# Down projection of a hybrid decoder layer: four units loaded and split in another order, their buffers on the other stack, and one operand sum moved from GpSimd to VectorE

## The chip, the cores and the metric

The kernel runs on one core of a Trainium2 chip. The metric is the device time of one execution in microseconds (us); less is better. Three executions of the kernel before took 1797.55, 1800.30 and 1800.89 us, the median is 1800.3.

## What is computed

One decoder layer on 1024 tokens of width 1024, all in float32. Two token mixers (sparse attention and latent attention) come first; the change does not touch them. Behind them stands the channel mixer, to which every edit belongs:

```python
h = _rmsnorm(x, g_pre_ffn[i])
u = _causal_dwconv(h @ w_up[i], w_conv[i], b_conv[i])   # (1024, 5632), 3 taps along the tokens
a, v = u[..., :D_FF], u[..., D_FF:]                     # D_FF = 2816
x = x + _rmsnorm((jax.nn.gelu(a) * v) @ w_down[i], g_post_ffn[i])
```

A gated embedding `w_ple_gate` ends the layer.

## The kernel before

**Arithmetic.** A float32 product is made of three passes of a rounded type: each operand is split into a high part (a copy on ScalarE, L198) and a low part (a subtraction on VectorE, L199), both by `split_evac`, and `mm3` issues high x high (L193), low x high (L194) and high x low (L195). So an operand is ready for TensorE only when ScalarE and then VectorE have been over it.

**Up projection.** The 2816 channels are 22 chunks of 128 (`NF`), each with two halves (gate and value). Chunk 0 is multiplied plainly; chunks 1 to 21 use the Strassen-Winograd scheme, seven products P1 to P7 instead of eight. Its right operands T1 to T4 are sums of blocks of h (T2 = B22 - T1, T3 = T2 - B11, T4 = B21 - T2). `t_blocks` (L1239) makes them once, behind chunk 0's products: T2 and T3 on VectorE through `total` (L1249), T4 on GpSimd (L1258, L1265), each in two halves of 128 x 1024, split by `put`. `hh`, `hl` are high and low parts of h, `rh`, `rl` those of a weight block, which `prep` splits (from `wraw` or a sum `S0` to `S3` made by `block_sum`, L1179). Each chunk's seven results are combined in VectorE into `C` (L1354 to L1370), and `conv_pieces` (L1278) applies the convolution: on each half one ScalarE instruction (L1285) and two taps on VectorE (L1289), then gelu, the product (L1296) and a store of 128 x 1024 to DRAM (`g_d`, L1297). The pieces of chunk f run among the products of chunk f+1; those of the last chunk run in a loop of their own behind the last product.

**Down projection.** Again seven products, in the order P1, P5, P6, P3, P7, P4, P2, over 11 units each (`UNITS`, 128 channels of `g_d` with their rows of `w_down`). `load(n)` issues a unit's transfers on SyncE's queue, `ready(n)` makes its sums on VectorE (L1435) and splits it into `whi`, `wlo`, and `down_product` (L1474) issues twelve matmuls a unit, three passes for each of four banks. It calls `ready(n + 4)` and `load(n + 7)` behind unit n. `QA` holds the units of P1, `QS` and `GB` those of P5 and the sums for P6, P3 and P7. Split units have four homes in turn: two in `W.parts`, two in `ring2`.

**Memory and order.** Buffers come from pools on two stacks, left and right; a pool that is opened over a closed one has to wait for the readers of what stood there. In the kernel before, `ep` (C, u) and `ring` (split weights) on the left and `tp`, `hp` (T blocks, h) on the right are closed behind the last convolution; then `yacc` (the sum of the output), `ring2` and `qs` are opened on the left and `qa` on the right (L1458 to L1464). A scheduler of the compiler sets the order of instructions on each engine from the order of the program, the pools and its own cost estimates, so an instruction may stand earlier on its engine than in the code: units 0 and 1 of the first down product, split behind the last convolution in the code, have their low words among the last up products on VectorE, at 1406.01 and 1409.54 us of the span. Within an engine the order is then fixed.

Of the kernel before, what the change touches and what calls it, by code (L numbers as in the profile page):

```python
# [18 lines left out]
D = 1024  # L19
# [5 lines left out]
NF = FF // 128  # L25
# [8 lines left out]
def dap(t, off, dims):  # L34
    return bass.AP(tensor=t.tensor, offset=t.offset + off, ap=[list(d) for d in dims])
# [130 lines left out]
def tile_hybrid_layer(ctx: ExitStack, tc: tile.TileContext, x, p, positions, g_pre_mix, w_in,  # L166
# [4 lines left out]
    nc = tc.nc  # L171
# [91 lines left out]
    g_d = [dram([128, T], F32, f"g_d{f}") for f in range(NF)]  # L263
# [30 lines left out]
    hp = Pool("hp", side="right")  # L294
# [351 lines left out]
    QA = [q0([128, 8, 512], F32R, "QA0"), q1([128, 8, 512], F32R, "QA1")]  # L646
# [444 lines left out]
    ps2 = Pool("ps2", space=PSUM)  # L1091
# [12 lines left out]
    ring = Pool("ring", side="left")  # L1104
# [29 lines left out]
    T1 = []  # L1134
# [64 lines left out]
    for t in (4, 5, 6, 7, 0, 1, 2, 3):  # L1199
        c, lt = t // 4, slice(t % 4 * 128, t % 4 * 128 + 128)  # L1200
# [37 lines left out]

    def t_blocks():  # L1239

        parts, t1, t2, b21 = [slice(0, 2), slice(2, 4)], T1, {}, {}

        def of(n, ks):
            return [f32(b[:, ks]) for b in BB[n]]

        def total(eng, tag, first, *rest):
            sum_ = W.parts([128, 2, 512], F32, tag, bufs=2)
            for op, b in rest:
                eng.tensor_tensor(sum_, first, b, op=op)  # L1249
                first = sum_  # L1250
            return sum_

        def put(n, ks, src):
            split_evac(BB[n][0][:, ks], BB[n][1][:, ks], src)

        for j, ks in enumerate(parts):
            b21[j] = ep([128, 2, 512], F32, "u", bufs=3)
            nc.gpsimd.tensor_tensor(b21[j], *of("B21", ks), op=OP.add)  # L1258
        for j, ks in enumerate(parts):
            put("T1", ks, t1[j])  # L1260
        for j, ks in enumerate(parts):
# [117 lines left out]
    DOWN = ("P1", "P5", "P6", "P3", "P7", "P4", "P2")  # L1379
    NJ = NF // 2  # L1380
    UNITS = [(p_, j) for p_ in DOWN for j in range(NJ)]
    QA, QS, GB, LOADED = {}, {}, {}, {}
    A_ = {"A11": (0, 0), "A12": (0, 1), "A21": (1, 0), "A22": (1, 1)}
    unit = {}

    def fetch(dst, name, j):

        r, c = int(name[1]) - 1, int(name[2]) - 1
        if name[0] == "A":
            nc.sync.dma_start(dst, g_d[c * NJ + j][:, r * 512:(r + 1) * 512])  # L1390
        else:
            nc.sync.dma_start(dst, dap(w_down, (r * NJ + j) * 128 * D + c * 512, [[D, 128], [1, 512]]))

    def temp():
        return wpool([128, 2, 512], F32, "wraw", bufs=3)

    def load(n):
        if n >= len(UNITS):
            return
        p_, j = UNITS[n]  # L1400
        if p_ == "P1":
            q = temp() if n < 3 else qa([128, 2, 512], F32, f"QA{j}")
            fetch(q[:, 0], "A11", j)
            fetch(q[:, 1], "B11", j)
            if n >= 3:
                QA[j] = q
        elif p_ == "P5":
            if j < 3:
                QA[j] = qa([128, 2, 512], F32, f"QA{j}")
                fetch(QA[j][:, 0], "A11", j)  # L1410
                fetch(QA[j][:, 1], "B11", j)
            q = QS[j] = qs([128, 2, 512], F32, f"QS{j}")
            GB[j] = qa([128, 512], F32, f"GB{j}")
            fetch(q[:, 1], "B12", j)
            fetch(GB[j], "A21", j)
            fetch(q[:, 0], "A22", j)
        elif p_ == "P7":
            q = QA[j]
        else:
            q = temp()  # L1420
            for i, name in enumerate({"P6": (None, "B22"), "P3": ("A12", "B22"), "P4": ("A22", "B21"),
                                      "P2": ("A12", "B21")}[p_]):
                if name:
                    fetch(q[:, i], name, j)
        LOADED[n] = q

    def ready(n):

        if n >= len(UNITS):
            return  # L1430
        p_, j = UNITS[n]
        q = LOADED.pop(n)

        def total(out_, a, b, op):
            nc.vector.tensor_tensor(out_, a, b, op=op)  # L1435

        sub, a, s = OP.subtract, QA.get(j), QS.get(j)
        if p_ == "P5":
            total(s[:, 1], s[:, 1], a[:, 1], sub)
            total(s[:, 0], GB[j], s[:, 0], OP.add)  # L1440
        elif p_ == "P6":
            total(s[:, 0], s[:, 0], a[:, 0], sub)
            total(s[:, 1], q[:, 1], s[:, 1], sub)
            q = s
        elif p_ == "P3":
            total(q[:, 0], q[:, 0], s[:, 0], sub)
        elif p_ == "P7":
            total(a[:, 0], a[:, 0], GB[j], sub)
            total(a[:, 1], s[:, 1], a[:, 1], sub)
        elif p_ == "P4":  # L1450
            total(q[:, 1], q[:, 1], s[:, 1], sub)
        pool = W.parts if n % 4 < 2 else ring2
        unit[n] = [pool([128, 2, 512], F32R, tag, bufs=2) for tag in ("whi", "wlo")]
        split_evac(*unit[n], q)
# [19 lines left out]
    def down_product(pi, per_unit):  # L1474
# [108 lines left out]
    for n, t in enumerate(ORDER):  # L1583
# [33 lines left out]
        else:  # L1617
# [45 lines left out]
```

## Time and profile before

| what | value |
|---|---|
| median of three executions | 1800.3 us |
| profiled execution | 1800.91 us, of which the span 1799.2 us |
| granted TensorE clock, mean | 0.984 |
| TensorE busy | 1728.0 us (96%) |
| VectorE busy | 1201.3 us (67%) |
| ScalarE busy | 838.8 us (47%) |
| GpSimd busy | 319.6 us (18%) |

TensorE is busy almost throughout, so time is found where it is idle or where its clock is below full speed. The positions of the stretches in the span: T blocks 1005 to 1060, the up projection's loop to 1438, the boundary to the down projection 1438 to 1458, the second and third down products 1463 to 1530. In the rows, PE is TensorE, DVE VectorE, ACT ScalarE, POOL GpSimd, SP SyncE and SPq its DMA queue; "x4" behind an operation joins four of them into one row.

### The profile page before, as it was taken

What the parts mean: (1) busy time and instruction counts of PE and PEld (TensorE: products, weight loads), DVE (VectorE), ACT (ScalarE), POOL (GpSimd) and SP (SyncE); (2) the same over time, 40 slices, a digit from 0 to 9 for tenths busy, and PEclk for the clock granted to TensorE, in tenths of its full rate; (3) what the DMA queues carried; (4) which work ended last, traced back from release to release, by engine and by line L of the source; (5) the groups of instructions that cost most, each with busy time, mean ns of one, the idle gap of its engine ahead of it and who ended that gap; (6) DMA issues with size and microseconds to landing.
All of it is one profiled execution on the core that took longest, in us unless ns stands there. A gap on an engine that the chain in (4) does not pass through costs nothing. (4 is left out here: it accounts for less than half of the span.)

```text
span 1799.2 us, 23461 instructions
## 1 busy us (share of the span) xinstructions
PE 1728.0 (96%) x8585; PEld 1414.3 (79%) x8585; DVE 1201.3 (67%) x1871; ACT 838.8 (47%) x1498; POOL 319.6 (18%) x471
## 2 busy tenths in 40 slices
PE   8989999999999999998999899999999979999998
PEld 7878888887787787887778678888888757887886
DVE  6544431117888787777764888888888679768443
ACT  6442322126777676676532434444444343335321
POOL 3132000004555543333211200000000000001010
PEclk8999999999999999999999999999999989999999
DMA  5394213310002226656462022232222282438111
GB/s 193 89 276 122 58 37 93 102 58 24 1 1 66 89 83 172 164 151 180 129 219 82 24 82 71 82 94 70 84 92 76 99 317 82 149 117 275 57 59 47
DMA packets 182511, 191.94 MB, mean 107 GB/s; under 512 B 12804, under 2 KB 136124, under 8 KB 182396
## 3 DMA queue, kind: packets, MB, share of 16 engines
q1 hardware_dynamic: 175292, 180.91, 32.6%
q10 hardware_dynamic: 7104, 9.54, 1.7%
q8 instruction: 68, 1.11, 0.3%
q14 instruction: 47, 0.39, 0.1%
HBM read 142.96 MB, written 47.45 MB: 106 GB/s over the span
## 5 line engine op out<-in xcount | busy, mean ns | idle before, releaser
L235 POOL TENSOR_SCALAR stat<-stat 128x1 f32<-128x1 f32 (+1 forms) x48 | 18.0, 374 | 892.0 <-ACT yn L1130 622.0
L198 ACT ACTIVATE ph<-pT 128x512 fp32r<-128x512 f32 (+1 forms) x244 | 130.4, 556 | 61.6 <-PE pT L734 53.8
L199 DVE TENSOR_TENSOR pl<-pT,ph 128x512 fp32r<-128x512 f32 (+1 forms) x244 | 149.6, 629 | 14.2 <-ACT ph L198 12.6
L193 PE MATMUL pT<-hh,whi 128*128 128x512 f32 x384 | 150.8, 393 | 2.7 <-DVE Vc L199 1.5
L195 PE MATMUL pT<-hh,wlo 128*128 128x512 f32 x384 | 150.4, 392 | 0.0
L194 PE MATMUL pT<-hl,whi 128*128 128x512 f32 x384 | 150.1, 391 | 0.0
L195 PE MATMUL big<-hh,rl 128*128 128x512 f32 x364 | 142.1, 391 | 3.6 <-DVE rl L199 3.6
L193 PE MATMUL big<-hh,rh 128*128 128x512 f32 x364 | 142.8, 393 | 2.5 <-ACT C L1352 1.4
L194 PE MATMUL big<-hl,rh 128*128 128x512 f32 x364 | 142.4, 391 | 0.0
L718 DVE TENSOR_REDUCE mx<-sc 128x1 f32<-128x640 f32 (+7 forms) x128 | 106.6, 835 | 34.4 <-PE sc L797 24.7
L107 DVE TENSOR_TENSOR wlo<-wraw,whi 128x1024 fp32r<-128x1024 f32 x26 | 31.9, 1226 | 138.3 <-ACT whi L106 138.1
L1289 DVE SCALAR_TENSOR_TENSOR u<-C,wcT,u 128x1024 f32<-128x1024 f32 x88 | 110.8, 1279 | 4.7 <-ACT u L1285 4.7
L194 PE MATMUL big<-wlo,whi 128*128 128x512 f32 x242 | 98.4, 407 | 9.0 <-DVE wlo L199 9.0
L193 PE MATMUL big<-whi 128*128 128x512 f32 x242 | 93.2, 401 | 9.8 <-ACT whi L198 9.8
L195 PE MATMUL big<-whi,wlo 128*128 128x512 f32 x242 | 96.4, 398 | 0.0
L198 ACT ACTIVATE rh<-S 128x512 fp32r<-128x512 f32 x84 | 52.5, 628 | 92.1 <-PE big L194 78.8
L193 PEld LDWEIGHTS pT<-hh,whi 128*128 128x128 f32 x384 | 72.5, 189 | 18.7 <-DVE Vc L199 1.6
L198 ACT ACTIVATE rh<-wraw 128x512 fp32r<-128x512 f32 x67 | 41.8, 630 | 92.4 <-PE big L194 44.2
L195 PEld LDWEIGHTS pT<-hh,wlo 128*128 128x128 f32 x384 | 72.4, 189 | 15.4
L194 PEld LDWEIGHTS pT<-hl,whi 128*128 128x128 f32 x384 | 72.5, 189 | 15.0
L195 PEld LDWEIGHTS big<-hh,rl 128*128 128x128 f32 x364 | 68.8, 189 | 18.4 <-DVE rl L199 4.0
L193 PEld LDWEIGHTS big<-hh,rh 128*128 128x128 f32 x364 | 68.6, 189 | 18.5 <-ACT C L1352 2.3
(485 smaller groups left out, 4791.9 us busy)
## 6 DMA issues: line engine op xcount, KB each, us to landing
wraw<-in_w_up_dram SPq DMA_DIRECT2D x44, 512.0 KB, 3.8
wraw<-in_w_in_dram SPq DMA_DIRECT2D x24, 512.0 KB, 4.2
g<-gm_d SPq DMA_DIRECT2D x48, 256.0 KB, 3.5
wraw<-in_w_down_dram SPq DMA_DIRECT2D x47, 256.0 KB, 3.2
g_d<-u SPq DMA_DIRECT2D x22, 512.0 KB, 3.4
wraw<-g_d SPq DMA_DIRECT2D x36, 256.0 KB, 3.0
xt<-in_x_dram SPq DMA_DIRECT2D x16, 512.0 KB, 7.0
gm_d<-gms ACTq DMA_DIRECT2D x16, 512.0 KB, 3.0
```

Of the source, the lines that this page charges most:

```text
L107: nc.vector.tensor_sub(lo, raw, f32(hi))
L193: nc.tensor.matmul(ps, lh, rh, start=start, stop=False, skip_group_check=more)
L194: nc.tensor.matmul(ps, lh, rl, start=False, stop=False, skip_group_check=more)
L195: nc.tensor.matmul(ps, ll, rh, start=False, stop=stop, skip_group_check=more)
L198: nc.scalar.activation(hi, ps, AF.Copy)
L199: nc.vector.tensor_sub(lo, ps, f32(hi))
L235: nc.gpsimd.tensor_scalar(st, st, EPS, None, op0=OP.add)
L718: nc.vector.tensor_reduce(u.nm[:, r:r + 1], src, axis=AX.XY, op=OP.max, negate=True)
L1289: nc.vector.scalar_tensor_tensor(u[s], C[s][:, 2 - sh:2 - sh + T], wcT[:, 2 - sh, ch:ch + 1], u[s], op0=OP.mult, op1=OP.add)
```

## The change

Two edits. First, T4 is summed on VectorE by `total`, as T2 and T3 are, in the buffers `whi`, `wlo` of `W.parts`; the four GpSimd instructions and their two `u` buffers go. T4's sum is now two instructions for each half, four in all.

Second, the down projection's functions move ahead of the up loop, and within the last chunk (f = 21) `load(0)` to `load(2)` are issued at the third product and `ready(0)`, `ready(1)` at the fifth and sixth. Behind the up loop only `tp` and `hp` are closed; `ring2`, `yacc` and `qa` are opened on the right, over them, all eleven `QA` at once in the order 0, 1, 2, 10, 3 to 9. The last convolution no longer stands ahead of the down projection: its pieces run behind units 0, 1 and 2 of the first down product, `ready` ahead of them, and `ep` and `ring` are closed behind unit 3, where `qs` and a new pool `gb` are opened on the left. `per_unit` is called ahead of `load(n + 7)`.

```diff
     def t_blocks():
-        for j, ks in enumerate(parts):
-            b21[j] = ep([128, 2, 512], F32, "u", bufs=3)
-            nc.gpsimd.tensor_tensor(b21[j], *of("B21", ks), op=OP.add)
...
             put("T2", ks, t2[j])
-            nc.gpsimd.tensor_tensor(b21[j], b21[j], t2[j], op=OP.subtract)
...
         for j, ks in enumerate(parts):
-            put("T4", ks, b21[j])
+            b21h, b21l = of("B21", ks)
+            put("T4", ks, total(nc.vector, ("whi", "wlo")[j], b21h, (OP.subtract, t2[j]), (OP.add, b21l)))
...
+            if f == NF - 1 and s == 2:
+                for i in range(3):
+                    load(i)
+            if f == NF - 1 and s in (4, 5):
+                ready(s - 4)
         pieces = conv_pieces(f, C)
-    for runs in pieces:
-        for run in runs:
-            run()
...
-    for n in range(3):
-        load(n)
-    for pl in (ep, ring, tp, hp):
+    for pl in (tp, hp):
         pl.close()
-    yp = Pool("yp", side="left")
+    ring2 = Pool("ring2", side="right")
+    yp = Pool("yp", side="right")
     yacc = yp([128, NT, D], F32, "yacc")
-    ring2 = Pool("ring2", side="left")
-    qs = Pool("qs", side="left")
     qa = Pool("qa", side="right")
+    for j in (0, 1, 2, 10) + tuple(range(3, 10)):
+        QA[j] = qa([128, 2, 512], F32, f"QA{j}")
     for n in range(3, 7):
         load(n)
-    for n in range(4):
+    for n in (2, 3):
         ready(n)
...
             ready(n + 4)
+            per_unit(j)
             load(n + 7)
-            per_unit(j)
...
-    for pi in range(5):
+    def last_conv(j):
+        nonlocal qs, gb
+        if j < 3:
+            for run in pieces[2 * j] + pieces[2 * j + 1]:
+                run()
+        if j == 3:
+            for pl in (ep, ring):
+                pl.close()
+            qs, gb = Pool("qs", side="left"), Pool("gb", side="left")
+
+    down_product(0, last_conv)
+    for pi in range(1, 5):
         down_product(pi, nothing)
```

**VectorE in the T stretch.** Each row is line, operation, what it writes from what, and its size; the digits behind a name tell buffers apart. `S` are weight sums, `rl` low words of weights, `C10` and `U3` parts of the combined result. In the kernel before, behind the last T3 split:

```order
L1179 TENSOR_TENSOR S2_10216<-wraw_9780,wraw_9870 128x512
L1360 TENSOR_TENSOR U2_10259<-one_10241,e1_10174 128x512
L1179 TENSOR_TENSOR S1_10192<-S0_10169,wraw_9780 128x512
L1296 TENSOR_TENSOR u_10218<-u_10171,u_10218 128x1024
L1362 TENSOR_TENSOR C10_9986<-big_10152,U2_10259 128x512
L1179 TENSOR_TENSOR S3_10238<-wraw_9780,S1_10192 128x512
L199 TENSOR_TENSOR rl_10255<-S1_10192,rh_10254 128x512
L199 TENSOR_TENSOR rl_10277<-S2_10216,rh_10276 128x512
L1363 TENSOR_TENSOR C10_9986<-C10_9986,U3_10220 128x512
L199 TENSOR_TENSOR rl_10298<-S0_10169,rh_10297 128x512
```

In the changed kernel (its lines are shifted: L1293 is the convolution's product, L1436 and L1437 are combinations):

```order
L1179 TENSOR_TENSOR S2_10216<-wraw_9780,wraw_9870 128x512
L1249 TENSOR_TENSOR whi_10142<-hh1_9059,whi_10122 128x1024
L1179 TENSOR_TENSOR S1_10192<-S0_10169,wraw_9780 128x512
L1249 TENSOR_TENSOR wlo_10147<-hh1_9059,wlo_10127 128x1024
L1293 TENSOR_TENSOR u_10218<-u_10171,u_10218 128x1024
L1436 TENSOR_TENSOR C10_9986<-big_10152,U2_10259 128x512
L1249 TENSOR_TENSOR whi_10142<-whi_10142,hl1_9060 128x1024
L1179 TENSOR_TENSOR S3_10238<-wraw_9780,S1_10192 128x512
L199 TENSOR_TENSOR rl_10255<-S1_10192,rh_10254 128x512
L1249 TENSOR_TENSOR wlo_10147<-wlo_10147,hl1_9060 128x1024
L199 TENSOR_TENSOR rl_10277<-S2_10216,rh_10276 128x512
L199 TENSOR_TENSOR rl_10298<-S0_10169,rh_10297 128x512
```

The same kinds of rows stand there still (the order of a few has turned), and among them the four new sums of T4, at L1249.

**VectorE at the boundary between the projections.** `wlo` from `wraw` is unit 2 of the first down product, from `QA3` unit 3, from `QA4` unit 4. Before:

```order
L1354 TENSOR_TENSOR C10_9986<-big_13110,U2_13151 128x512
L1289 SCALAR_TENSOR_TENSOR u_13230<-C10_9986,wcT_85,u_13230 128x1024
L1289 SCALAR_TENSOR_TENSOR u_13235<-C11_9987,wcT_85,u_13235 128x1024
L1289 SCALAR_TENSOR_TENSOR u_13230<-C10_9986,wcT_85,u_13230 128x1024
L1289 SCALAR_TENSOR_TENSOR u_13235<-C11_9987,wcT_85,u_13235 128x1024
L199 TENSOR_TENSOR wlo_13310<-QA4_13270,whi_13309 128x1024
L199 TENSOR_TENSOR wlo_13329<-QA5_13273,whi_13328 128x1024
L1296 TENSOR_TENSOR u_13235<-u_13230,u_13235 128x1024
L199 TENSOR_TENSOR wlo_13288<-wraw_13247,whi_13287 128x1024
L199 TENSOR_TENSOR wlo_13292<-QA3_13267,whi_13291 128x1024
```

After (L1286 is a tap, L1293 the product, L1428 the combination):

```order
L1428 TENSOR_TENSOR C10_9986<-big_13110,U2_13151 128x512
L199 TENSOR_TENSOR wlo_13279<-wraw_13180,whi_13278 128x1024
L1286 SCALAR_TENSOR_TENSOR u_13304<-C10_9986,wcT_85,u_13304 128x1024
L1286 SCALAR_TENSOR_TENSOR u_13327<-C11_9987,wcT_85,u_13327 128x1024
L1286 SCALAR_TENSOR_TENSOR u_13304<-C10_9986,wcT_85,u_13304 128x1024
L199 TENSOR_TENSOR wlo_13283<-QA3_13263,whi_13282 128x1024
L1286 SCALAR_TENSOR_TENSOR u_13327<-C11_9987,wcT_85,u_13327 128x1024
L199 TENSOR_TENSOR wlo_13301<-QA4_13264,whi_13300 128x1024
L199 TENSOR_TENSOR wlo_13324<-QA5_13265,whi_13323 128x1024
L1293 TENSOR_TENSOR u_13327<-u_13304,u_13327 128x1024
```

Unit 2's low words move from behind the four taps and the product to a place ahead of them, and unit 3's to a place ahead of the last tap.

**VectorE in the second down product.** Between the low words of its units 3 and 4 (`QS3`, `QS4`), before:

```order
L199 TENSOR_TENSOR wlo_13529<-QS3_13463,whi_13528 128x1024
L1435 TENSOR_TENSOR QA0_13389<-QA0_13389,GB0_13393 128x512
L1435 TENSOR_TENSOR QA0_13389<-QS0_13392,QA0_13389 128x512
L199 TENSOR_TENSOR wlo_13559<-QS4_13486,whi_13558 128x1024
L1435 TENSOR_TENSOR QS2_13440<-QS2_13440,QA2_13437 128x512
L1435 TENSOR_TENSOR QS2_13440<-wraw_13694,QS2_13440 128x512
L1435 TENSOR_TENSOR QA1_13413<-QA1_13413,GB1_13417 128x512
L1435 TENSOR_TENSOR QA1_13413<-QS1_13416,QA1_13413 128x512
L1435 TENSOR_TENSOR QS3_13463<-QS3_13463,QA3_13267 128x512
L1435 TENSOR_TENSOR QS3_13463<-wraw_13714,QS3_13463 128x512
L199 TENSOR_TENSOR wlo_13582<-QS5_13509,whi_13581 128x1024
```

After:

```order
L199 TENSOR_TENSOR wlo_13532<-QS3_13466,whi_13531 128x1024
L1355 TENSOR_TENSOR QS5_13512<-GB5_13513,QS5_13512 128x512
L1355 TENSOR_TENSOR QS2_13443<-QS2_13443,QA2_13261 128x512
L1355 TENSOR_TENSOR QS2_13443<-wraw_13697,QS2_13443 128x512
L1355 TENSOR_TENSOR QS6_13535<-QS6_13535,QA6_13266 128x512
L1355 TENSOR_TENSOR QA1_13260<-QA1_13260,GB1_13421 128x512
L1355 TENSOR_TENSOR QA1_13260<-QS1_13420,QA1_13260 128x512
L1355 TENSOR_TENSOR QS6_13535<-GB6_13536,QS6_13535 128x512
L1355 TENSOR_TENSOR QS7_13565<-QS7_13565,QA7_13267 128x512
L199 TENSOR_TENSOR wlo_13562<-QS4_13489,whi_13561 128x1024
```

Between `QS3` and `QS4` two sums became eight, those of the units and products that follow; before, they stood further behind.

## Rows read from the trace of the kernel before

**Rows 1.** The page's first line.

```profile
span 1799.2 us, 23461 instructions
```

**Rows 2.** Busy time by stretch: us of each engine (instructions), granted clock, DMA.

```profile
1005.00:1060.00 55.00, 44.78 (x174) 33.98 (x172) 54.85 (x56) 28.65 (x36) 10.98 (x4) 0.94 0.16 48
1100.00:1420.00 320.00, 320.00 (x1413) 265.00 (x1413) 267.97 (x348) 144.51 (x200) 0.00 (x0) 1.00 0.26 85
1438.00:1458.00 20.00, 9.65 (x27) 6.59 (x26) 12.55 (x11) 8.27 (x8) 0.00 (x0) 0.66 1.03 380
1463.00:1530.00 67.00, 62.35 (x264) 48.40 (x263) 66.79 (x92) 27.38 (x30) 0.00 (x0) 1.00 0.38 132
```

**Rows 3.** Timeline of PE, 1010 to 1060: start, us, operation [idle before <-releaser].

```profile
1018.53 0.54 PE L195 MATMUL big<-hh,rl 128*128 128x512 f32 x1 [3.60 <-DVE rl L199]
...
1056.57 0.50 PE L193 MATMUL one<-T3h,rh 128*128 128x512 f32 x1 [1.47 <-DVE C L1370]
```

**Rows 4.** Timeline of POOL, 1004 to 1023.

```profile
1005.04 5.06 POOL L1258 TENSOR_TENSOR u<-hh,hl 128x1024 f32<-128x1024 f32 x2 [4.62 <-DVE hl L199]
1014.73 3.20 POOL L1265 TENSOR_TENSOR u<-u,whi 128x1024 f32<-128x1024 f32 x1 [4.63 <-DVE whi L1249]
```

**Rows 5.** Timeline of DVE, 1004 to 1024.

```profile
1004.87 0.42 DVE L1150 TENSOR_TENSOR whi<-whi,hl 128x256 f32<-128x256 f32 x1
1005.20 2.62 DVE L1150 TENSOR_TENSOR wlo<-wlo,hl 128x256 f32<-128x256 f32 x1
1007.75 3.43 DVE L1249 TENSOR_TENSOR whi<-hh,whi 128x1024 f32<-128x1024 f32 x1
1011.10 1.21 DVE L1249 TENSOR_TENSOR wlo<-hh,wlo 128x1024 f32<-128x1024 f32 x1
...
1015.64 2.83 DVE L199 TENSOR_TENSOR rl<-wraw,rh 128x512 fp32r<-128x512 f32 x1
...
1020.14 3.42 DVE L1249 TENSOR_TENSOR whi<-whi,hh 128x1024 f32<-128x1024 f32 x1
```

**Rows 6.** Timeline of PE, 1437 to 1458.

```profile
1437.94 0.39 PE L195 MATMUL big<-hh,rl 128*128 128x512 f32 x1
1446.21 1.22 PE L193 MATMUL big<-whi 128*128 128x512 f32 x2 [7.87 <-ACT whi L198]
1449.91 0.79 PE L194 MATMUL big<-wlo,whi 128*128 128x512 f32 x1 [2.48 <-DVE wlo L199]
...
1457.90 0.39 PE L193 MATMUL big<-whi 128*128 128x512 f32 x1
```

**Rows 7.** Timeline of DVE and ACT, 1438 to 1444.

```profile
1438.44 0.69 DVE L1354 TENSOR_TENSOR C<-big,U 128x512 f32<-128x512 f32 x1 [5.80 <-PE big L195]
...
1439.17 2.37 ACT L1285 ACTIVATE u<-C,wcT 128x1024 f32<-128x1024 f32 x2 [3.91 <-DVE C L1354]
...
1440.44 4.87 DVE L1289 SCALAR_TENSOR_TENSOR u<-C,wcT,u 128x1024 f32<-128x1024 f32 x4 [1.31 <-ACT u L1285]
...
1441.45 1.99 ACT L198 ACTIVATE whi<-QA 128x1024 fp32r<-128x1024 f32 x2
```

**Rows 8.** Timeline of SP's queue and of DVE, 1448 to 1464.

```profile
1448.75 0.32 SPq L1297 DMA_DIRECT2D g_d<-u  x1
...
1463.21 0.69 DVE L1435 TENSOR_TENSOR QS<-QS,QA 128x512 f32<-128x512 f32 x1 [6.32 <-DMA QS<-in_w_down_dram]
```

**Rows 9.** Timeline of DVE, 1478 to 1481.

```profile
1478.76 1.22 DVE L199 TENSOR_TENSOR wlo<-QS,whi 128x1024 fp32r<-128x1024 f32 x1
1479.90 0.69 DVE L1435 TENSOR_TENSOR QS<-QS,QA 128x512 f32<-128x512 f32 x1
1480.50 0.69 DVE L1435 TENSOR_TENSOR QS<-GB,QS 128x512 f32<-128x512 f32 x1
```

**Rows 10.** Who PE waited for, 1463 to 1530: us in total, times, longest.

```profile
PE big L194 <- DVE wlo L199: 4.2, 6, 1.1
PE big L193 <- ACT whi L198: 0.5, 1, 0.5
```

More of the change, by code (lines that the diff above doesn't have):

```diff
@@ L1239, in t_blocks @@
     def t_blocks():
-        parts, t1, t2, b21 = [slice(0, 2), slice(2, 4)], T1, {}, {}
+        parts, t1, t2 = [slice(0, 2), slice(2, 4)], T1, {}
         def of(n, ks):
@@ L1300, in conv_pieces, with fetch @@
                 [lambda: tap(1, 1)], [lambda: tap(1, 2)], [out_], []]
+    DOWN = ("P1", "P5", "P6", "P3", "P7", "P4", "P2")
+    NJ = NF // 2
+    UNITS = [(p_, j) for p_ in DOWN for j in range(NJ)]
+    QA, QS, GB, LOADED = {}, {}, {}, {}
+    A_ = {"A11": (0, 0), "A12": (0, 1), "A21": (1, 0), "A22": (1, 1)}
+    unit = {}
+    def fetch(dst, name, j):
+        r, c = int(name[1]) - 1, int(name[2]) - 1
+        if name[0] == "A":
+            nc.sync.dma_start(dst, g_d[c * NJ + j][:, r * 512:(r + 1) * 512])
+        else:
+            nc.sync.dma_start(dst, dap(w_down, (r * NJ + j) * 128 * D + c * 512, [[D, 128], [1, 512]]))
@@ new lines, in temp, with load @@
+    def temp():
+        return wpool([128, 2, 512], F32, "wraw", bufs=3)
+    def load(n):
+        if n >= len(UNITS):
+            return
+        p_, j = UNITS[n]
+        if p_ == "P1":
+            q = temp() if n < 3 else QA[j]
+            fetch(q[:, 0], "A11", j)
+            fetch(q[:, 1], "B11", j)
+        elif p_ == "P5":
+            if j < 3:
+                fetch(QA[j][:, 0], "A11", j)
+                fetch(QA[j][:, 1], "B11", j)
+            q = QS[j] = qs([128, 2, 512], F32, f"QS{j}")
+            GB[j] = gb([128, 512], F32, f"GB{j}")
+            fetch(q[:, 1], "B12", j)
+            fetch(GB[j], "A21", j)
+            fetch(q[:, 0], "A22", j)
+        elif p_ == "P7":
+            q = QA[j]
+        else:
+            q = temp()
+            for i, name in enumerate({"P6": (None, "B22"), "P3": ("A12", "B22"), "P4": ("A22", "B21"),
+                                      "P2": ("A12", "B21")}[p_]):
+                if name:
+                    fetch(q[:, i], name, j)
+        LOADED[n] = q
@@ new lines, in ready, with total @@
+    def ready(n):
+        if n >= len(UNITS):
+            return
+        p_, j = UNITS[n]
+        q = LOADED.pop(n)
+        def total(out_, a, b, op):
+            nc.vector.tensor_tensor(out_, a, b, op=op)
+        sub, a, s = OP.subtract, QA.get(j), QS.get(j)
+        if p_ == "P5":
+            total(s[:, 1], s[:, 1], a[:, 1], sub)
+            total(s[:, 0], GB[j], s[:, 0], OP.add)
+        elif p_ == "P6":
+            total(s[:, 0], s[:, 0], a[:, 0], sub)
+            total(s[:, 1], q[:, 1], s[:, 1], sub)
+            q = s
+        elif p_ == "P3":
+            total(q[:, 0], q[:, 0], s[:, 0], sub)
+        elif p_ == "P7":
+            total(a[:, 0], a[:, 0], GB[j], sub)
+            total(a[:, 1], s[:, 1], a[:, 1], sub)
+        elif p_ == "P4":
+            total(q[:, 1], q[:, 1], s[:, 1], sub)
+        pool = W.parts if n % 4 < 2 else ring2
+        unit[n] = [pool([128, 2, 512], F32R, tag, bufs=2) for tag in ("whi", "wlo")]
+        split_evac(*unit[n], q)
@@ L1370, in tile_hybrid_layer @@
                 nc.vector.tensor_tensor(C[1][:, low], seven, U2, op=OP.add)
-        pieces = conv_pieces(f, C)
-    for runs in pieces:
-        for run in runs:
-            run()
[L1379 to L1454, printed above, removed]
@@ L1511, in nothing @@
         pass
-    for pi in range(5):
+    qs = gb = None
+    def last_conv(j):
+        nonlocal qs, gb
+        if j < 3:
+            for run in pieces[2 * j] + pieces[2 * j + 1]:
[6 more added lines that the diff above has]
+    for pi in range(1, 5):
         down_product(pi, nothing)
-    qa.close()
+    for pl in (qa, gb):
+        pl.close()
     wgp = Pool("wgp", side="right")
@@ L1633, in tile_hybrid_layer @@
                 nc.sync.dma_start(out[0, ts, hs], X3[t][:, hs])
-    for pl in (pp, ring2, yp, W.parts, fp, wgp, ps2, dram, wpool, consts):
+    for pl in (pp, W.parts, fp, wgp, yp, ring2, ps2, dram, wpool, consts):
         pl.close()
```

## The prediction

> **What bounds the kernel now.** I read the page's span first [rows 1]: 1799.2 us, 1.7 below the profiled execution's own 1800.91. Every saving below is made against that execution, which lies 0.6 above the median of 1800.3; so a saving s gives 1800.3 - s for the median.
>
> Then I read busy time by stretch [rows 2]. In the up loop, 1100 to 1420, PE works 320.00 of 320.00 us at full clock, 1413 matmuls, so 0.2265 us each and 12 x 0.2265 = 2.72 us for a unit of the down projection. VectorE is at 267.97 there, with room. Nothing that is moved inside that loop can gain. Three stretches have idle PE and belong to the change: the T blocks (44.78 of 55, so 10.2 idle, clock 0.94), the boundary between the projections (9.65 of 20, clock 0.66), and the second and third down products (62.35 of 67). In the first and third VectorE is at 54.85 of 55 and 66.79 of 67: there VectorE is the bound and PE waits for it. At the boundary VectorE itself has 12.55 of 20, so there a chain of waits counts, not a sum of work.
>
> **T4 on VectorE.** Removed: four GpSimd sums [rows 4], two at once from 1005.04 in 5.06 us, then 3.20 from 1014.73 and another like it near 1020. The reader is to see what VectorE does in the same time [rows 5]. An L1150 sum of 128x256 takes 0.42 at 1004.87, and the next of the same shape, started with GpSimd's first sum running, 2.62. An L1249 sum of 128x1024 takes 1.21 at 1011.10 and 3.43, 3.42 at 1007.75 and 1020.14. An `rl` subtraction of 128x512 takes 2.83 at 1015.64 where sums of that size take 0.69 [rows 7, 8]. Four VectorE instructions are longer by 2.20, 2.22, 2.14 and 2.21, together 8.8 us, one for each GpSimd sum. That is the price of the GpSimd sums on VectorE. Added: four L1249 sums of 128x1024, at the start-to-start distance of that size, 1479.90 - 1478.76 = 1.14 [rows 9], 4.56 us. Net: VectorE has 8.8 - 4.6 = 4.2 us less.
>
> Ahead of the combination L1370 on which PE waits last there (1.47 at 1056.57, [rows 3]), VectorE's queue holds the same instructions as before and these four; so that wait ends 4.2 earlier. PE's earlier waits (3.60 at 1018.53 [rows 3], and shorter ones) fall away and gather into one or two longer ones; the work of PE in between is shorter than VectorE's, so the end is set by VectorE either way. What I can't read is the clock: behind each long wait PE's granted clock drops (0.94 in the stretch, 0.06 x 55 = 3.3 us lost in all), and another long wait may cost half of that, 1.7. Ends: 4.2 - 1.7 = 2.5, and 4.5 if a slow part goes as well. I take 3.5.
>
> The Trainium skill speaks against this edit: "Perfetto Trace Analysis", section "Optimizing Scalar/DVE Operations", says that with a saturated VectorE it may make sense to offload some work to ScalarE or even GpSimd, and here VectorE is saturated and the work goes the other way. The same paragraph warns that the two share a read port of the memory, so that offloading between them might not help; the trace agrees with the warning by the four lengthened instructions. By the first sentence alone the stretch would pay the four sums in full, which is rival B.
>
> **The boundary.** Before, the chain is this. P3's last matmul starts at 1437.94 [rows 6] and ends near 1438.2. The combination follows at 1438.44 (0.69), ScalarE's two `u` from 1439.17 (2.37), four taps in 4.87 from 1440.44 [rows 7]. PE idles 7.87 us to 1446.21 and 2.48 to 1449.91, and unit 4 starts at 1457.90 [rows 6]. Without a stall units 2 and 3 would take 2 x 2.72, and unit 4 would start at 1443.6: 14.3 us are lost, idle and slow clock together.
>
> After, units 2 and 3 live on the right, over T and h blocks, not over the convolution's buffers. The first home is free with the last matmul that reads those blocks. By the order of the queues: ScalarE copies unit 2 (1.99 for two [rows 7], so 1.0) from 1438.3 to 1439.3; VectorE, which has done the combination by 1439.1, takes its low words to 1440.5, then three taps (4.87/4 = 1.22 each) to 1444.1, unit 3's low words to 1445.25, the last tap, unit 4's to 1447.6, unit 5's to 1448.7 and the product to 1449.9. PE waits 1.1 for unit 2's high words and 0.7 for its low ones, works 2.7 at full clock, waits some 2 for unit 3, and starts unit 4 between 1447.5 (full clock) and 1449.5 (the slow clock that the stretch now shows). I take 1448.5. Gain 1457.9 - 1448.5 = 9.4, from 8.4 to 10.4.
>
> Units 0 and 1 stand in the last up products already, so their new place in the code is worth nothing; the up loop's VectorE has room for what moves. The store of the last chunk is issued near 1450 in place of 1448.75 [rows 8], since the product stands behind more splits. `QS` and `GB` queue behind it on SyncE. Before, the first sum on `QS` came 1463.21 - 1448.75 = 14.5 us behind that store, but nine `GB` transfers of 5.8 us stood between them; now `QS0` is next in the queue. So I let it land before VectorE comes to it, and keep the 14.5 as the worse end: then the first sum starts at 1464.5 where the queue would allow 1460.8, and 3.7 us of the gain go.
>
> **What is late next: the second product's sums.** Between the low words of `QS3` and `QS4` there are now eight sums in place of two, and so on: the sums of P6 and P7 stand ahead of splits that PE needs at once. From the low words of `QS0` to those of `QS4` of the third product I count 61 sums and 15 splits. A sum costs 1480.50 - 1479.90 = 0.60, a split 1.14 [rows 9]: 36.6 + 17.1 = 53.7 us. PE consumes those 15 units in 15 x 2.72 = 40.8. With unit 4 starting at time S, unit 10's split waits for its home until unit 6 ends, S + 8.2; three sums and `QS0`'s split end at S + 14.0, and PE wants them 0.7 into unit 11, at S + 7 x 2.72 + 0.7 = S + 19.7. The lead is 5.7. Loss: 53.7 - 40.8 - 5.7 = 7.2. Before, PE lost 4.2 + 0.5 = 4.7 in this place [rows 10], which goes with the old order. Net loss 2.5; with the late transfer 6.2. Behind about 1530 every engine has the instructions in the same order as before, so nothing more follows.
>
> **Sum.** 9.4 - 2.5 + 3.5 = 10.4, so 1800.91 - 10.4 = 1790.5 for the profiled execution and 1800.3 - 10.4 = 1789.9 for the median, rounded to 1790. The terms' ends give 8.4 - 6.2 + 2.5 = 4.7 and 10.4 - 2.5 + 4.5 = 12.4; with a third of the P5 and P6 loss not coming, 14. So the likeliest's own range is 1786 to 1795.6.
>
> **Rivals.**
> A, more than that: VectorE makes up time in the down products (sums that are early take less time from the splits), and PE's slow clock in the T stretch goes wholly. Then 9.4 + 4.7 + 4.2 + 3.3 = 21.6, time 1779. For it: PE's waits in P5 and P6 are short and many [rows 10]. Against: both stretches have a full VectorE [rows 2].
> B, VectorE pays the T4 sums on the path: if the long instructions of [rows 5] are long for another reason, the added 4.6 stands where 4.2 was to go. 1800.3 - 6.9 + 4.6 = 1798.0. Against: four GpSimd sums and four long instructions, pairwise at the same time.
> C, the change does not do what it says at the boundary, since units 0 and 1 were early before: units 2 and 3 still end behind the taps, and only T4 counts. 1800.3 - 3.5 = 1796.8. Against: the queue order of VectorE, where unit 2's low words stand ahead of the taps.
> D, slower: the last convolution, moved into the first down product, makes the store and so all `QS` late, and VectorE starves PE through P5 and P6. Each us by which `QS0`'s low words come later than S + 14.0 is lost. It decides from 10.4 + 3.6 = 14 us later (10.4 use up the gain, 3.6 reach the bound below), so a first sum 25 us behind the store, not 14.5. At 15 us late, 1790 + 15 = 1805. For it: VectorE waited 6.32 for that transfer before [rows 8]. Against: the queue ahead of it is shorter now.
>
> **Numbers.** 0.2% is 3.6 us, about what a measurement of this kernel can tell from no change: same is 1796.7 to 1803.9. Chances: forecast 0.72, A 0.09, B 0.06, C 0.08, D 0.05. Faster: forecast but for 0.02, A, and 0.07 for the parts of B and C that fall below 1796.7, about 0.86; same 0.10; slower 0.04. The range holds the forecast and touches C: 1783 to 1797.
>
> **What would show it.** In the profile after: no GpSimd sum at 1005 to 1023 and no VectorE instruction there of 2.6 us or more; PE's last wait in that stretch ending some 4 us sooner. At the boundary no wait of 7.9 us, unit 2 starting within 2 us of the last up matmul, unit 4 about 11 us behind it and no more than 13. In P5 and P6 waits for low words of 6 to 8 us in all, where 4.7 stood. The prediction is wrong if PE waits there for a transfer, if the taps still come ahead of unit 2, or if the clock stays low for more than some 4 us in either stretch.

## The result

The changed kernel takes 1792.48 us (median of five executions, 1789.08 to 1793.26) against 1800.3: the ratio is 0.9948, with a 95% interval of 0.9925 to 0.9971, so 5.2 to 13.5 us are gained. Run again later on, it took 1787.72, ratio 0.9919 (0.9903 to 0.9936). A ratio is taken over all executions of both kernels, so it differs a little from the quotient of the two medians. The forecast was 1790, with 1783 to 1797 as its range.

The profiled execution took 1793.26, of which the span 1791.5. The same four stretches as in [rows 2] (columns: us, busy us and instructions of PE, PEld, DVE, ACT and POOL, granted clock, DMA share, GB/s):

```profile
1005.00:1060.00 55.00, 47.23 (x194) 36.39 (x193) 52.00 (x64) 29.34 (x37) 0.27 (x3) 0.96 0.16 48
1100.00:1420.00 320.00, 319.54 (x1410) 264.31 (x1409) 270.23 (x351) 145.95 (x201) 0.00 (x0) 1.00 0.26 85
1438.00:1458.00 20.00, 16.75 (x65) 12.72 (x64) 14.81 (x13) 11.00 (x11) 0.00 (x0) 0.91 0.97 339
1463.00:1530.00 67.00, 61.79 (x258) 48.48 (x257) 64.96 (x90) 27.12 (x30) 0.00 (x0) 0.97 0.42 150
```

At the boundary PE's busy time goes from 9.65 to 16.75 of 20 us and the clock from 0.66 to 0.91. The T stretch has 2.45 more, the last stretch 0.56 less, and its clock is no longer full. The up loop is what it was. The stretches are cut at the same times in both kernels, while the work in them has moved (P3's last matmul starts at 1440.25, not at 1437.94), so these rows say where to look; what a stretch is worth is taken from matmul numbers below.

**The T stretch.** PE's longer waits there, which answer to [rows 3]:

```profile
1037.69 0.50 PE L195 MATMUL big<-hh,rl 128*128 128x512 f32 x1 [0.97 <-DVE rl L199]
...
1045.24 0.79 PE L195 MATMUL one<-T2h,rl 128*128 128x512 f32 x1 [2.23 <-DVE rl L199]
...
1057.65 0.50 PE L193 MATMUL one<-T3h,rh 128*128 128x512 f32 x1 [2.33 <-DVE C L1444]
```

VectorE, answering to [rows 5]:

```profile
1010.18 0.41 DVE L1150 TENSOR_TENSOR whi<-whi,hl 128x256 f32<-128x256 f32 x1
1010.51 0.42 DVE L1150 TENSOR_TENSOR wlo<-wlo,hl 128x256 f32<-128x256 f32 x1
1010.85 1.22 DVE L1249 TENSOR_TENSOR whi<-hh,whi 128x1024 f32<-128x1024 f32 x1
1011.99 1.22 DVE L1249 TENSOR_TENSOR wlo<-hh,wlo 128x1024 f32<-128x1024 f32 x1
...
1016.53 0.68 DVE L199 TENSOR_TENSOR rl<-wraw,rh 128x512 fp32r<-128x512 f32 x1
...
1018.87 1.22 DVE L1249 TENSOR_TENSOR whi<-whi,hh 128x1024 f32<-128x1024 f32 x1
```

Of the four long instructions of 2.62, 3.43, 2.83 and 3.42 none is left: they take 0.42, 1.22, 0.68 and 1.22. GpSimd has 0.27 us in the stretch where it had 10.98.

**The boundary.** PE, answering to [rows 6]; the first row is unit 2's first matmuls, the third falls in unit 3, the last begins unit 4:

```profile
1441.56 0.73 PE L193 MATMUL big<-whi 128*128 128x512 f32 x2 [0.92 <-ACT whi L198]
1442.82 0.50 PE L194 MATMUL big<-wlo,whi 128*128 128x512 f32 x1 [0.53 <-DVE wlo L199]
...
1447.62 0.54 PE L194 MATMUL big<-wlo,whi 128*128 128x512 f32 x1 [1.80 <-DVE wlo L199]
...
1451.60 0.63 PE L193 MATMUL big<-whi 128*128 128x512 f32 x2
```

The waits of 7.87 and 2.48 are now 0.92, 0.53 and 1.80. VectorE there, answering to [rows 7]:

```profile
1440.75 0.69 DVE L1428 TENSOR_TENSOR C<-big,U 128x512 f32<-128x512 f32 x1 [5.80 <-PE big L195]
1441.54 1.22 DVE L199 TENSOR_TENSOR wlo<-wraw,whi 128x1024 fp32r<-128x1024 f32 x1
1442.75 3.68 DVE L1286 SCALAR_TENSOR_TENSOR u<-C,wcT,u 128x1024 f32<-128x1024 f32 x3
1446.34 1.22 DVE L199 TENSOR_TENSOR wlo<-QA,whi 128x1024 fp32r<-128x1024 f32 x1
1447.48 1.28 DVE L1286 SCALAR_TENSOR_TENSOR u<-C,wcT,u 128x1024 f32<-128x1024 f32 x1
1448.67 2.36 DVE L199 TENSOR_TENSOR wlo<-QA,whi 128x1024 fp32r<-128x1024 f32 x2
1450.94 1.22 DVE L1293 TENSOR_TENSOR u<-u 128x1024 f32<-128x1024 f32 x1
```

Unit 2's low words stand ahead of the taps (L1286), unit 3's ahead of the last tap, and PE's wait of 1.80 ends with these low words of unit 3. The store and the first sum on `QS`, answering to [rows 8], on SyncE's queue:

```profile
1452.19 0.33 SPq L1294 DMA_DIRECT2D g_d<-u  x1
```

and on VectorE:

```profile
1462.22 0.68 DVE L1355 TENSOR_TENSOR QS<-QS,QA 128x512 f32<-128x512 f32 x1
```

No transfer is waited for: the sum starts as the split ahead of it ends, 10.0 us behind the store where it was 14.5. In the second and third products, answering to [rows 10] (who PE waited for; us, times, longest):

```profile
PE big L194 <- DVE wlo L199: 5.2, 4, 2.4
```

**By the number of the matmul.** All 8585 matmuls are in each trace, in an order that differs by a few neighbours only. So the time between two numbers (counted from 0) can be taken in every trace, and a stretch is compared free of the time that was lost or won ahead of it. Matmul 7100 is P3's last; 7124 is the last of unit 3; 7440 stands in unit 30, past the last of PE's waits in the third product. The columns are the kernels of the next section; "again" is the changed kernel's second profile. Microseconds between the starts:

| kernel | 400 to 700, attention | 5250 to 5460, T stretch | 5700 to 7100, up loop | 7100 to 7124, boundary | 7124 to 7440, units 4 to 30 | 7800 to 7950 |
|---|---|---|---|---|---|---|
| before | 65.98 | 63.51 | 318.32 | 19.73 | 79.18 | 40.50 |
| changed | 73.39 | 60.55 | 318.31 | 11.12 | 80.65 | 37.75 |
| changed, again | 67.93 | 60.66 | 318.32 | 9.56 | 80.65 | 38.77 |
| T4 alone | 70.08 | 60.82 | 318.32 | 19.33 | 79.33 | 38.32 |
| second edit alone | 64.43 | 63.45 | 318.32 | 9.54 | 79.61 | 38.01 |
| taps first | 64.48 | 60.63 | 318.32 | 16.16 | 76.88 | 37.10 |
| sums in order | 66.21 | 60.71 | 318.32 | 9.56 | 71.63 | 39.62 |
| convolution spread | 67.13 | 60.56 | 318.31 | 7.46 | 71.63 | 39.62 |
| before, sums in order | 64.35 | 63.49 | 318.32 | 20.11 | 71.63 | 38.85 |
| taps first, sums in order | 67.55 | 60.80 | 318.32 | 15.95 | 71.63 | 39.06 |

The three stretches of the change give 2.96 + 8.61 - 1.47 = 10.1 us in the first pair of profiles, and with the second profile 2.85 + 10.17 - 1.47 = 11.6.

### The profile page after: what moved, and what is told of

Its sections match the earlier page's. It is cut to its first block, busy times and chain, and to the rows that moved or that the text cites. A ratio compares the mean times of both kernels' runs of the same rounds, so it can differ in the third digit from the quotient of the medians.

```text
span 1791.5 us, 23480 instructions
## 1 busy us (share of the span) xinstructions
PE 1724.0 (96%) x8585; PEld 1411.1 (79%) x8585; DVE 1196.9 (67%) x1875; ACT 837.7 (47%) x1498; POOL 308.5 (17%) x467
## 3 DMA queue, kind: packets, MB, share of 16 engines
q10 hardware_dynamic: 7104, 9.54, 1.7%
## 4 chain that ended last, share of the span: by engine, by line
PE 77%; DVE 8%; DMA 7%; ACT 3%; issue 2%; POOL 1%; SPq 1%; ACTq 0%; DVEq 0%; POOLq 0%
PE big L194 9%; PE big L193 9%; PE big L195 9%; PE pT L193 7%; PE pT L195 7%; PE pT L194 7%; PE pT L734 5%; PE one L193 3%; PE one L194 3%; PE one L195 3%; PE oT L744 3%; PE oT L743 3%; PE sc L797 1%; DVE wlo L199 1%; PE sc L790 1%
## 5 line engine op out<-in xcount | busy, mean ns | idle before, releaser
L1286 DVE SCALAR_TENSOR_TENSOR u<-C,wcT,u 128x1024 f32<-128x1024 f32 x88 | 110.8, 1278 | 3.4 <-ACT u L1282 3.4
L194 PEld LDWEIGHTS pT<-hl,whi 128*128 128x128 f32 x384 | 72.8, 190 | 15.1
```

The lines of the kernel that those rows point to most:

```text
L194: nc.tensor.matmul(ps, lh, rl, start=False, stop=False, skip_group_check=more)
```

## The experiments

Each was timed in five rounds beside the kernel before, whose median was 1801.78 us on the chip of the first four and 1802.81 on that of the last four.

**T4 alone** (the kernel before with `t_blocks` of the changed one).

```diff
-            nc.gpsimd.tensor_tensor(b21[j], b21[j], t2[j], op=OP.subtract)
-            put("T4", ks, b21[j])
+            put("T4", ks, total(nc.vector, ("whi", "wlo")[j], b21h, (OP.subtract, t2[j]), (OP.add, b21l)))
```

> The kernel before with the first edit alone: T4 summed on VectorE, the down projection as it was. Theory (the GpSimd sums lengthen VectorE's instructions by 8.8 us in all, the four sums on VectorE cost 4.6): the wait for the last combination of the T stretch ends some 3 to 4 us sooner, no VectorE instruction there of 2.6 us or more, the boundary's wait of 7.9 us stays; time 1800.3 - 3.0 = 1797.3, from 1796 to 1798.5. Rival (the four sums are paid on VectorE's path, and what the T stretch gained in the changed kernel comes from elsewhere): 1800.3 to 1805, and long VectorE instructions remain.

Measured: 1800.73 us, ratio 0.9985 (0.9967 to 1.0003), 2.7 us less with an interval from 5.9 less to 0.5 more. By time alone that is not told from no change; the number expected was missed, and 1800.73 lies in the rival's span. The trace has what the theory asked for: VectorE's instructions at the same place are short,

```profile
1011.75 0.42 DVE L1150 TENSOR_TENSOR wlo<-wlo,hl 128x256 f32<-128x256 f32 x1
1012.08 1.22 DVE L1249 TENSOR_TENSOR whi<-hh,whi 128x1024 f32<-128x1024 f32 x1
...
1017.76 0.69 DVE L199 TENSOR_TENSOR rl<-wraw,rh 128x512 fp32r<-128x512 f32 x1
...
1020.10 1.22 DVE L1249 TENSOR_TENSOR whi<-whi,hh 128x1024 f32<-128x1024 f32 x1
```

the T stretch takes 60.82 against 63.51, which is 2.7 less, and the boundary stays:

```profile
1450.06 1.22 PE L193 MATMUL big<-whi 128*128 128x512 f32 x2 [7.87 <-ACT whi L198]
```

**The second edit alone** (the changed kernel with T4 on GpSimd, the same lines the other way round).

> The changed kernel with T4 summed on GpSimd as before: the second edit alone. Theory: the long VectorE instructions of 2.6 to 3.4 us are back in the T stretch, the boundary is as in the changed kernel (unit 4 starts about 11 us behind the last up product, not 20), the second and third down products lose some 6 us; time 1792.5 + 3.0 = 1795.5 from the changed kernel, or 1800.3 - 8.8 + 1.6 = 1793.1 from the kernel before; 1792.5 to 1796.5. Rival (the boundary brings nothing that lasts, the gain is T4's): 1798 or more.

Measured: 1789.28 us, ratio 0.994 (0.9916 to 0.9963), below the expected span. That span started from the changed kernel's first median, 1792.5, which lies 4.8 above its second. Against the kernel before, the stretches say 0.06 + 10.19 - 0.43 = 9.8 us, the ratio 0.006 x 1801.78 = 10.8. On VectorE the four long instructions are back,

```profile
1004.47 2.62 DVE L1150 TENSOR_TENSOR wlo<-wlo,hl 128x256 f32<-128x256 f32 x1
1007.01 3.43 DVE L1249 TENSOR_TENSOR whi<-hh,whi 128x1024 f32<-128x1024 f32 x1
...
1014.91 2.83 DVE L199 TENSOR_TENSOR rl<-wraw,rh 128x512 fp32r<-128x512 f32 x1
...
1019.40 3.41 DVE L1249 TENSOR_TENSOR whi<-whi,hh 128x1024 f32<-128x1024 f32 x1
```

each beside a GpSimd sum:

```profile
1004.30 5.06 POOL L1258 TENSOR_TENSOR u<-hh,hl 128x1024 f32<-128x1024 f32 x2 [4.62 <-DVE hl L199]
1013.99 3.20 POOL L1265 TENSOR_TENSOR u<-u,whi 128x1024 f32<-128x1024 f32 x1 [4.63 <-DVE whi L1249]
1019.02 2.71 POOL L1265 TENSOR_TENSOR u<-u,wlo 128x1024 f32<-128x1024 f32 x1 [1.83 <-DVE wlo L1249]
```

So the length of these four belongs to the GpSimd sums: it comes and goes with them, the four instructions themselves being the same. The last three of the four end 1.08, 0.55 and 1.08 us behind the end of a GpSimd sum (1009.36, 1017.19, 1021.73), a little less than they take when undisturbed (1.22, 0.68, 1.22): these rows suggest that each was held until the sum had ended and did its own work then. This agrees with the warning in the Trainium skill ("Perfetto Trace Analysis", section "Optimizing Scalar/DVE Operations") that the two engines share a read port and offloading between them might not help: here it cost 8.8 us of VectorE to save 4.6.

**Taps first** (the changed kernel, units 2 and 3 split behind the last convolution's four taps; `taps[f]` keeps the last tap's instruction).

```diff
+    for runs in pieces:
+        for run in runs:
+            run()
...
     for n in (2, 3):
-        ready(n)
+        with tc.issue_after(taps[NF - 1]):
+            ready(n)
```

> The changed kernel, but the low words of units 2 and 3 queued on VectorE behind the four last convolution taps; buffers stay where the change put them. Theory (what the boundary gained is the place of unit 2's low words in VectorE's queue, which the homes on the right stack allow): PE waits some 6 us longer for unit 2's low words, unit 4 starts 3 to 6 us later, time 1795.5 to 1798.5. Rival (the buffers' place alone gains, by letting ScalarE's copies and transfers go early): within 1 us of the changed kernel, 1792.5.

Measured: 1791.25 us (1783.79 to 1799.84), ratio 0.9947 (0.9928 to 0.9966). The theory's time was missed, and the figure is 1.25 below 1792.5, so by time alone the rival would be nearer. The trace shows otherwise. PE waits 6.52 for unit 2's low words,

```profile
1435.14 0.73 PE L193 MATMUL big<-whi 128*128 128x512 f32 x2 [0.92 <-ACT whi L198]
1442.39 0.80 PE L194 MATMUL big<-wlo,whi 128*128 128x512 f32 x1 [6.52 <-DVE wlo L199]
```

which come when VectorE is through with the taps:

```profile
1436.33 4.87 DVE L1288 SCALAR_TENSOR_TENSOR u<-C,wcT,u 128x1024 f32<-128x1024 f32 x4 [1.31 <-ACT u L1284]
1441.12 1.22 DVE L199 TENSOR_TENSOR wlo<-wraw,whi 128x1024 fp32r<-128x1024 f32 x1
```

The boundary takes 16.16 where it was 11.12 and 9.56, so 5.0 to 6.6 are lost where the theory had 3 to 6. Against the 19.73 of the kernel before, 3.6 are still gained, with the taps first: ScalarE's copy comes early, and PE's wait for unit 2's high words is 0.92, not 7.87. The stretch behind takes 76.88 where it was 80.65, so 3.8 come back. One reading is that VectorE is the bound behind unit 4, and a later unit 4 only shortens the waits that follow. But the edit also left the scheduler another order of the sums there: between the low words of `QS3` and `QS4` stand five sums (1473.86 to 1478.00 in this trace), where the changed kernel has eight. How much of the 3.8 is the later start and how much the order isn't shown; the last experiment fixes the order.

**Sums in order** (the changed kernel; `lows[n]` keeps unit n's low split).

```diff
         def total(out_, a, b, op):
-            nc.vector.tensor_tensor(out_, a, b, op=op)
+            with tc.issue_after(lows[n - 2]):
+                nc.vector.tensor_tensor(out_, a, b, op=op)
```

> The changed kernel, with the sums of every unit of the down projection queued on VectorE behind the low words of the unit two before it, so that the sums of the third and later products can't pass the splits of the second. Theory (PE waits in the second and third products because VectorE does sums there that are not yet wanted; in program order a unit needs two sums and a split, 2 x 0.60 + 1.14 = 2.34 us of VectorE against 2.72 of PE): the 6 us of waits for low words between 1463 and 1530 fall to 1 or less, time 1792.5 - 5.5 = 1787, from 1785 to 1788.5. Rival (the second product waits for its transfers or for free homes, or the sums come late in the later products instead): 1791 to 1795.

Measured: 1783.02 us, ratio 0.9897 (0.9875 to 0.992), better than expected. From unit 4 to matmul 7440 PE loses nothing: 71.63 us for 316 matmuls, 0.2267 each. A stretch of 68 us behind unit 4, in this kernel

```profile
1448.00:1516.00 68.00, 68.00 (x301) 56.33 (x301) 58.04 (x72) 30.34 (x33) 0.00 (x0) 1.00 0.56 192
```

and in the changed one:

```profile
1454.00:1522.00 68.00, 62.79 (x262) 49.33 (x261) 62.27 (x86) 27.11 (x30) 0.00 (x0) 0.97 0.54 184
```

PE is full in place of 62.79, with VectorE at 58.04. The gain is 80.65 - 71.63 = 9.0: the four waits of 5.2, some 1.7 behind the longest of them, where seven matmuls start 0.43 apart and others 0.32 to 0.34 in place of 0.227, and the rest in matmuls that start 0.27 to 0.34 apart behind the other waits or in a stall too short to be listed. The expectation had counted the waits alone.

**The convolution spread** (sums in order, and besides):

```diff
         if j < 3:
-            for run in pieces[2 * j] + pieces[2 * j + 1]:
-                run()
+            with tc.issue_after(lows[j + 4]), tc.issue_after(highs[j + 4]):
+                for run in sum(([pieces[0]], [pieces[2], pieces[3], pieces[1]], [pieces[4], pieces[5]])[j], []):
+                    run()
```

> The kernel with the sums in program order (the run before this one of that kind took 1783.0, ratio 0.9897), and besides the last convolution spread out: ScalarE's and VectorE's parts of it are queued behind the split of the unit four ahead, so that units 2, 3 and 4 are split first and then one or two taps stand between splits. Theory (what is left at the boundary are PE's waits for unit 3's high and low words behind the convolution on ScalarE and VectorE, 1.8 us and the slow clock behind it): unit 4 starts 7 to 8 us behind the first of the last matmuls counted where it was 9.6 to 11.1, time 1783.0 - 2 to 3.5 = 1779.5 to 1781. Rival (the later store of the last chunk makes the second product's transfers late): 1783 or more, with waits at the start of the second product.

Measured: 1780.19 us, ratio 0.9871 (0.9853 to 0.989): the fastest, and as expected. Of the boundary's waits these are left:

```profile
1440.63 0.73 PE L193 MATMUL big<-whi 128*128 128x512 f32 x2 [0.92 <-ACT whi L198]
1441.89 0.50 PE L194 MATMUL big<-wlo,whi 128*128 128x512 f32 x1 [0.53 <-DVE wlo L199]
```

and the stretches there and in the products behind have full clock:

```profile
1438.00:1458.00 20.00, 18.55 (x81) 14.75 (x80) 17.01 (x15) 12.32 (x12) 0.00 (x0) 1.00 0.84 296
1463.00:1530.00 67.00, 67.00 (x298) 55.47 (x297) 60.30 (x78) 31.39 (x34) 0.00 (x0) 1.00 0.52 182
```

**The kernel before with its sums in order** (the same edit of `total` on the kernel before).

> The kernel before with only the order of the down projection's sums pinned, as in the run that took 1783.0. Theory (the waits of the second and third products have the same cause before the change, and are not bound to the boundary): from the start of unit 4 on, PE loses nothing until the third product has ended, 7.6 us less by the trace, time 1801.8 - 7 = 1795, from 1793 to 1796.5. Rival (before the change it is the late transfers that make PE wait there, so the order brings nothing): 1799 to 1802.

Measured: 1796.88 us, ratio 0.9967 (0.9952 to 0.9982), 5.9 us less and 0.4 above the theory's upper end. The stretch behind unit 4 takes 71.63, the boundary's 20.11 stays:

```profile
1461.00:1532.00 71.00, 71.00 (x315) 58.76 (x314) 59.54 (x72) 31.85 (x35) 0.00 (x0) 1.00 0.41 146
```

So the waits of [rows 10] go with the order too. The transfer for which VectorE waited 6.32 [rows 8] had a share in them, but only by the order. In the kernel before, low words of the first product stood behind that wait and four sums, though ScalarE had written their high words by 1459.16, and PE waited for them:

```profile
1465.79 1.22 DVE L199 TENSOR_TENSOR wlo<-QA,whi 128x1024 fp32r<-128x1024 f32 x1
1467.06 0.50 PE L194 MATMUL big<-wlo,whi 128*128 128x512 f32 x1 [0.62 <-DVE wlo L199]
```

With the sums pinned, such low words come first, and the first sum starts 8.1 us behind matmul 7124 where it was 5.5. What else the wait of 6.32 cost before, where VectorE is full behind it, isn't shown; with the sums pinned PE loses nothing.

**The changed kernel again**, unchanged.

> The changed kernel once more, to have its trace twice. Theory (the 7 us by which its first profile lies behind the kernel before's at 130 us of the span are chance of the execution, since no instruction is moved there): the stretch from the 400th to the 700th matmul takes anything from 64 to 74 us; T stretch 60.6 from the 5250th to the 5460th matmul, boundary 9.5 to 11.1 to unit 4. Rival (the changed kernel is slower there by its own): 73 us again. Time 1789 to 1793.5.

Measured: 1787.72 us, 1.3 below the span expected. The stretch from matmul 400 to 700 takes 67.93 in this profile and 73.39 in the first, with 65.98 in that of the kernel before, so most of the 7 us are chance of the execution. From 100 to 135 us, the first profile of the changed kernel,

```profile
100.00:135.00 35.00, 26.72 (x125) 20.81 (x124) 12.61 (x21) 12.31 (x20) 11.14 (x21) 0.93 0.84 226
```

the second,

```profile
100.00:135.00 35.00, 28.70 (x138) 24.01 (x138) 14.44 (x24) 14.08 (x23) 11.63 (x22) 0.95 0.95 258
```

and that of the second edit alone, with the same instructions there:

```profile
100.00:135.00 35.00, 31.43 (x155) 25.17 (x154) 15.84 (x28) 14.94 (x23) 11.66 (x24) 1.00 1.01 284
```

PE is busy for 26.72, 28.70 and 31.43 us; the clock is 0.93, 0.95 and 1.00, the DMA share 0.84, 0.95 and 1.01. Whether the transfers are late and the clock follows, or what else starts it, was not tried.

At the boundary the two profiles have the same waits but another clock. The second has

```profile
1448.10 0.50 PE L194 MATMUL big<-wlo,whi 128*128 128x512 f32 x1 [1.78 <-DVE wlo L199]
```

where the first has 1.80. Behind it, first profile and second:

```profile
1447.00:1452.00 5.00, 4.38 (x12) 3.47 (x13) 5.00 (x5) 1.79 (x3) 0.00 (x0) 0.66 1.05 387
1447.00:1452.00 5.00, 3.90 (x17) 3.23 (x18) 5.00 (x5) 3.14 (x4) 0.00 (x0) 1.00 1.05 388
```

**Taps first, with the sums in order.**

> Sums in program order (1783.0) and the low words of units 2 and 3 behind the four taps. Theory (with the sums out of order VectorE is the bound from the boundary through the third product, so that a later start of unit 4 is partly given back there; with the sums in order PE is the bound behind unit 4, so nothing is given back): 5 to 6.6 us slower than 1783.0, 1788 to 1790. Rival (the taps' place costs little, as the time with the sums out of order suggests, 1791.25 against 1792.5): 1782 to 1785.

Measured: 1786.27 us, ratio 0.9912 (0.9897 to 0.9927), against 0.9897 without the taps first. That is 0.0015 x 1802.81 = 2.7 us, or 3.3 by the medians; it lies between the theory's span and the rival's, and the intervals overlap, so the time doesn't decide. The trace speaks for the theory: the same wait at the boundary,

```profile
1448.21 0.80 PE L194 MATMUL big<-wlo,whi 128*128 128x512 f32 x1 [6.52 <-DVE wlo L199]
```

15.95 us there against 9.56, and 71.63 behind it, so nothing of the 6.4 is given back where the sums are pinned in both. The two profiled executions are 9.5 us apart. Why the median shows only half of the 6.4 is open; the early stretch, which varies by 9 us among the ten profiles, is enough for it.

## Why the prediction was right, point by point

**T4.** Right in its mechanism and nearly in its size. From the first `hl` split of the stretch to the last combination VectorE took 1055.84 - 1003.00 = 52.84 us before and 1056.90 - 1008.32 = 48.58 after, 4.26 less, where 4.2 was worked out from 8.8 and 4.6. PE kept 2.96 of it by matmul number; the rest, 1.3, was lost behind its last wait, 2.33 at 1057.65, where six matmuls start 0.43 apart; 0 to 1.7 had been allowed, and I took about half. Two things in it were wrong. I had PE's waits gather into one or two; seven are left, two of them over 2 us. And one sign that was to tell of an error, a clock that stays low for more than some 4 us, did come in this stretch: the granted clock is 0.66 from 1045 to 1050, 0.88 from 1055 to 1060 and 0.78 from 1060 to 1065, behind the waits of 2.23 and 2.33, which makes 6.8 us at half speed, in two parts, and 10.2 in the second profile. The kernel before had 6.8 there too, behind 3.60 and 2.21. What the clock cost behind the last wait, 1.3, was still within what had been allowed.

**The boundary.** Right: 8.61 and 10.17 in two profiles, with 9.4 forecast and 8.4 to 10.4 as its ends. The two profiles differ by the clock, which fell behind the wait of 1.80 in one of them. The waits came as listed: 0.92 and 0.53 for 1.1 and 0.7, 1.80 for 2. The taps-first kernel parts the gain: with the buffers where the change put them, but the low words behind the taps, 3.6 of it stay, and the place in VectorE's queue is worth the other 5.0 to 6.6. So the order makes the larger part, and the buffers' place, which lets ScalarE's copy come early, the rest.

**The second and third products.** The cause was right, the term mis-sized. The lead was right: `QS0`'s low words were worked out for 14.0 us behind unit 4's start and came at 1465.93 - 1451.60 = 14.3. But the forecast compared waits with waits, 7.2 against 4.7. Measured against a full PE (71.63), the changed kernel loses 9.0, of which only 5.2 are waits, and the kernel before 79.18 - 71.63 = 7.6, of which 4.7 are waits. The difference is 1.5 where 2.5 was forecast: a wait costs more than its own row, by the slower matmuls behind it, and I had charged this on neither side. That the net came so near is luck in part: the loss after was put 1.8 too low and the loss before 2.9 too low, and the two errors cancel to within 1.0. As waits alone the loss after is 5.2, below the 6 to 8 that were to be seen.

**The rivals.** B is refuted by the traces of the T4-alone and second-edit-alone kernels (60.82 and 63.45 in the T stretch), C by the latter, which gains 9.8 by its stretches without T4. D fell with the first sum 10.0 us behind the store. A did not come by itself: the slow clock of the T stretch stayed, and VectorE's early sums made PE lose more. What it spoke of was there, though: the waits in the second and third products could be had, by the order of the sums.

**The sum.** 10.4 was forecast, and the stretches give 10.1 and 11.6. The medians give 7.8 (1800.3 to 1792.48) in the first comparison and 15.1 (1802.81 to 1787.72) in the second, the ratios 9.4 and 14.6. In the first pair of profiles, whose spans are 7.6 apart, the rest lies where no instruction was changed: ahead of matmul 4880 the changed kernel's profile was 7.4 us longer, from 4880 to 5250 it was 2.05 shorter, and from 7800 to 7950 2.75 shorter. So the range was needed for a reason that the prediction did not name: chance in stretches that no edit touches. That 1790 lies between the two medians is in part luck, since this chance is as large as the gain.

## What to carry to other kernels

Where two engines slow each other, price an instruction by what its neighbour loses: four GpSimd sums cost VectorE 8.8 us and saved it 4.6. When a scheduler places work that is ready early, look whether it stands ahead of work that the bounding engine waits for; here pinning sums behind splits gave 9 us, as much as the change's own boundary, with VectorE's work unchanged. And where chance elsewhere is as large as the gain, subtract starts of the same instruction, stretch by stretch, ahead of believing a median; look then, too, whether an edit in one stretch has changed the order in the next.

## What was not expected of the hardware

The same instructions, with the same order, took 64.35 to 73.39 us from the 400th to the 700th matmul in ten profiles, while the up loop's 1400 matmuls took 318.31 to 318.32 in all ten. In the two longest (73.39, and 70.08 in T4 alone) the granted clock was 0.83 from 110 to 120 us, where it was 1.00 in the kernel before, with the DMA share at 0.82 against 0.96, and in the first of them with waits of PE of 1 to 2 us for VectorE and ScalarE. And with a wait of 1.80 at the same place the boundary took 11.12 us in one execution and 9.56 in another, by the clock behind it.
